# A hybrid block on one core: three raw weight buffers instead of two, and high priority for the copies between seven half-size products

## The chip, the core and the metric

The kernel runs on one core of a Trainium2 chip. The metric is the time of one execution in device microseconds (us), the median of several. The core has engines that work side by side, each through its own queue of instructions in a fixed order: PE (TensorE, matrix products; its weight loads are listed as PEld), DVE (VectorE), ACT (ScalarE), POOL (GpSimd) and SP (SyncE, which here only issues transfers). Engines wait for each other through semaphores. A page or an answer of the profile writes "A <- B" for "A stood idle until B was done".

## The reference

528 tokens (16 learnt meta tokens and 512 inputs) of width 1024 go through one block. With `z = rms_norm(h) @ w_in` cut into eight parts:

```python
u_rnn, u_gate, q, k, v, g_ret, ga, gb = jnp.split(z, IN_SPLITS, axis=-1)
xr = causal_dwconv(u_rnn, rnn_conv_w[l], rnn_conv_b[l])
hr = rg_lru(xr, ...)                      # recurrence over time, width 1280
o_a = hr * jax.nn.gelu(u_gate)
o = retention(rotary(q), rotary(k) * RET_DK ** -0.5, v)   # 4 heads, keys 256, values 512
o_b = head_rms(o) * jax.nn.silu(g_ret)
mixed = sigmoid(ga) * (o_a @ w_branch_rnn) + sigmoid(gb) * (o_b @ w_branch_ret)
h = h + mixed @ w_out
up = causal_dwconv(rms_norm(h) @ w_up, fconv_w, fconv_b)
gate, val = jnp.split(up, 2, axis=-1)
h = h + (gelu(gate) * val) @ w_down
out = rms_norm(h)[:, N_META:]
```

Everything is float32, and the weights come to some 100 MB. Their products are what the time goes into.

## The kernel before, in words

**Products.** PE multiplies in float16. Each float32 matrix is split in a high part (rounded to float16) and a low part (what is left), and a product is the sum of three: high by high, high by low and low by high. The split of a tile is two instructions in `split` (L91 to L94): ACT writes the high part (L92) and DVE the low one (L93), after ACT. So each weight passes three stages before PE can use it: a transfer into a raw buffer, a split on ACT, a split on DVE.

**Weights as units.** The weights are cut into units of 128x2048 float32 (1 MB; those of `w_branch_rnn` 640 KB), listed in the order of their use. `unit_load` takes a tile `raw` from the pool `wraw` (L59, two buffers) and issues its transfer on SP through `load` (L98 to L104), which keeps all weight loads in the order in which they were asked for. The float16 tiles `wt` (128x2x1024) come from the pool `wsp` (L60, ten). A raw buffer is free again when DVE has split the last of it; the load that is to fill it waits for that at the head of SP's queue, and everything that SP has to issue behind it waits as well.

**When splits are issued.** The program calls `tick` at many places between products. Each call issues at most one step of the list, a split or the sums below, as long as the tiles needed for the units ahead don't pass `ahead`. `emit_step` (L292 to L297) first makes sure that raw loads have been asked for up to one unit past the unit whose step it issues (`u + 2`).

**Seven half-size products.** Twenty units (gates `g_ret`, `ga`, `gb`, and `w_branch_ret`) use a scheme with seven products of half-size blocks in place of eight. Their weights are prepared by `fast_steps` (L237 to L275): two cuts are split as they are (B11, then B21 with B22), then three additions on DVE change the raw buffer in place (L256 to L258), then two more cuts (T1 with T3, T4 with T2) are split from the result. `fast_products` (L859 to L902) does the seven products, in accumulators of 257 columns, `pa`, `pe` and `pb`:

1. B11 into `pa`; `keep` (L871, L872) copies `pa` to the first half of `kept` on ACT.
2. T3 into `pe`.
3. T2, added on top in `pa`; `keep` copies `pa` to the second half of `kept`.
4. B21 into `pb`, and an addition with `kept` on DVE (L889).
5. T1, added on top in `pa`; `keep` copies to `last`; an addition on DVE (L893).
6. B22, added on top in `pa`; the gate function reads it (L905).
7. T4, added on top in `pe`; an addition on DVE (L900), and the gate function of the other half.

So before the products 3, 5 and 6 PE has to wait until ACT has copied `pa`, and the product in between is what covers that copy. For a unit of gates a product is 12 matmuls of 128x128 by 128x257, for `w_branch_ret` 24. L867 is the line of all of these matmuls; their inputs are `xs` and `xh` for the gates and `ob` for the second branch, and `pm` (L418) is an ordinary product of the first branch, 60 matmuls, which are woven in between.

**The order of instructions.** Up to `order.close()` (L736) the instructions of PE, ACT and DVE stand in the order in which the program issues them. Behind that, a scheduler chooses for each engine among what is ready by its own estimate, in the order of the program unless a part is given high priority. What is ready depends on the buffers as well, so the number of raw buffers changes the order too.

**The run of the work.** Up to about 140 us come the norm, the recurrence's projections and the recurrence; to 230 us queries and keys with their rotary multiplications (L759 to L761); to 425 us scores, values, retention and the gates of heads 0 to 2 (`gated`); from 420 to 644 us the mix (`mix_unit`, `gate_unit` for head 3, `mix_products`); then `w_out` with the residual `h` (L1186 loads it, L1193 loads the gain `gffn`), the second norm, `w_up` with its convolutions, `w_down` and the last norm.

Of the kernel before, what the change touches and what calls it, by code (L numbers as in the profile page):

```python
# [10 lines left out]
AF = mybir.ActivationFunctionType  # L11
# [40 lines left out]
def hybrid_block_kernel(ctx, tc, x, meta, norm_mix_g, w_in, conv_w, conv_b, rg_a_w, rg_a_b,  # L52
                        rg_x_w, rg_x_b, lam, w_brnn, w_bret, w_out, norm_ffn_g, w_up,
                        fconv_w, fconv_b, w_down, norm_final_g, rope_t, decay_t, out):
    nc = tc.nc
    const = ctx.enter_context(tc.tile_pool(name="const", bufs=1))
    xp = ctx.enter_context(tc.tile_pool(name="xp", bufs=4))
    pieces = ctx.enter_context(tc.tile_pool(name="pieces", bufs=46))
    wraw = ctx.enter_context(tc.tile_pool(name="wraw", bufs=2))  # L59
    wsp = ctx.enter_context(tc.tile_pool(name="wsp", bufs=10))  # L60
    work = ctx.enter_context(tc.tile_pool(name="work", bufs=8))
    small = ctx.enter_context(tc.tile_pool(name="small", bufs=4))
# [11 lines left out]
    def acc(name):  # L74
        return psum["acc"].tile([P, 2, 512], F32, name=name, tag="acc")

    def bank(name):
        return psum["bank"].tile([P, 512], F32, name=name, tag="bank")
# [9 lines left out]
    def wtile(name):  # L88
        return work.tile([P, T], F32, name=name, tag="w")
# [17 lines left out]
    def kmaj(w, k0, nk, c0, ncol):  # L107
        return w[k0 * P:(k0 + nk) * P, c0:c0 + ncol].rearrange("(k p) c -> p k c", p=P)

    units = []  # L110

    def unit(nk, ncol, parts, fast=False):
        units.append((nk, ncol, parts, fast))
        return len(units) - 1
# [3 lines left out]
    for i in range(5):  # L118
        u = unit(8, 256, [(0, 0, kmaj(w_in, 0, 8, o_ur + 256 * i, 256))])
# [65 lines left out]
    loaded = []  # L185

    def unit_load(cuts=1):

        nk, ncol, parts, fast = units[len(loaded)]
        raw = wraw.tile([P, 2048], F32, name="raw")  # L190
        n = nk * ncol
        rv = raw[:, :n].rearrange("p (k c) -> p k c", k=nk)
        for k0, c0, ap in parts:
            load(rv[:, k0:k0 + ap.shape[1], c0:c0 + ap.shape[2]], ap)
        loaded.append(len(loaded))
        if fast:
            return fast_steps(rv, nk // 2, ncol // 2)
        hk = nk // 2
        hn = hk * ncol
        tiles = []  # L200

        def step(i, c):
            def run():
                if c == 0:
                    tiles.append(wsp.tile([P, 2, 1024], F16, name="wt"))
                sl = slice(c * hn // cuts, (c + 1) * hn // cuts)
                split(tiles[i][:, 0, sl], tiles[i][:, 1, sl], raw[:, i * hn:(i + 1) * hn][:, sl], SW)
            return run

        wviews.append(lambda a, k, c0, m: tiles[k // hk][:, a, k % hk * ncol + c0:k % hk * ncol + c0 + m])  # L210
        return [step(i, c) for i in range(2) for c in range(cuts)]
# [66 lines left out]
    last_keep = [None]  # L278
# [12 lines left out]

    def emit_step():  # L292
        u, run = steps[done[0]]
        while len(loaded) < min(u + 2, len(units)):
            queue(unit_load())
        run()
        done[0] += 1  # L297

    def queue(new):
        steps.extend((len(loaded) - 1, run) for run in new)  # L300

    def get(u):
        current[0] = max(current[0], u)
        while len(loaded) <= u:
            queue(unit_load())
        while done[0] < len(steps) and steps[done[0]][0] <= u:
            emit_step()
        return wviews[u]

    def tick(n=1, late=True):  # L310


        for _ in range(n):
            if done[0] == len(steps):
                if len(loaded) == len(units):
                    return
                queue(unit_load())
            u = steps[done[0]][0]
            if sum(unit_tiles(i) for i in range(current[0], u + 1)) > ahead[0]:
                return  # L320
            if gating[0] and not late and hasattr(steps[done[0]][1], "late"):
                return
            emit_step()
# [292 lines left out]
    def conv_product(n):  # L616
        u, col = u_ur[n]
        if n in early:
            ps = early.pop(n)
            project_half(ps, get(u), col, xf, HR, 1)  # L620
        else:
            ps = acc("ps")
            project(ps, get(u), col, xf, HR, KD)
        return ps
# [46 lines left out]
    for n in range(NR):  # L671
        ps = conv_product(n)
# [41 lines left out]
    for n in range(NR):  # L714
        ps = acc("ps")
        u, col = u_ug[n // 2], (n % 2) * P
# [142 lines left out]
    def fast_products(ws, src, func, finish):  # L859


        last_k = 4 * len(ws) - 1

        def product(ps, wf, xf_, first=False):
            for k in range(last_k + 1):
                for aw, ax in SPLIT:
                    nc.tensor.matmul(ps[:, :257], ws[k // 4](wf, aw, k % 4), src(xf_, ax, k),  # L867
                                     start=first and k == 0 and (aw, ax) == (0, 0), stop=k == last_k and aw == 1,
                                     skip_group_check=True)

        def keep(dst, ps):  # L871
            last_keep[0] = nc.scalar.activation(dst, ps[:, :257], AF.Copy).ins  # L872

        kept, last = wtile("kept"), wtile("last")
        g0, g1 = wtile("g0"), wtile("g1")
        h0, h1 = slice(0, 257), slice(257, TQ)
        pa = bank("pa")
        product(pa, "B11", "A11", True)
        keep(kept[:, h0], pa)
        yield  # L880
        pe = bank("pe")
        product(pe, "T3", "F7", True)
        yield
        product(pa, "T2", "F6")
        keep(kept[:, h1], pa)
        yield
        pb = bank("pb")
        product(pb, "B21", "A12", True)
        nc.vector.tensor_tensor(g0[:, h0], pb[:, :257], kept[:, h0], op=ALU.add)  # L889
        yield  # L890
        product(pa, "T1", "F5")
        keep(last[:, h0], pa)
        nc.vector.tensor_tensor(g1[:, h1], pe[:, :257], last[:, h0], op=ALU.add)  # L893
        yield
        product(pa, "B22", "F3")
        func(g1[:, h0], pa[:, :257], -1.0, 0)
        func(g1[:, h1], g1[:, h1], -1.0, 257)
        finish(1, g1)
        product(pe, "T4", "A22")
        nc.vector.tensor_tensor(g0[:, h1], pe[:, :257], kept[:, h1], op=ALU.add)  # L900
        func(g0[:, :TQ], g0[:, :TQ], 1.0, 0)
        finish(0, g0)  # L902
# [215 lines left out]
    def branch(us, src, nk):  # L1118
        ps = acc("pm")
        project(ps, get(us.pop(0)), 0, src, HH, nk)  # L1120
        tick(2)
        return ps[:, :, :257]
# [21 lines left out]
    for i in range(2):  # L1144
# [5 lines left out]
        ps = branch(u_ba, oa_of, NR)  # L1150
# [525 lines left out]
```

## Time and profile before

| | |
|---|---|
| median of three runs | 1068.25 us (1067.45 to 1068.45) |
| the profiled execution, first to last instruction (span) | 1066.5 us |
| PE busy | 1048.0 us, 98% of the span |
| DVE busy | 853.2 us, 80% |
| ACT busy | 587.9 us, 55% |
| granted TensorE clock | 1.00 in all stretches, 0.99 in the last |
| bytes read | 108.04 MB, 103 GB/s over the span |

For the profiled execution itself nothing but its span is known, which is 1.75 us under the median. A row of a timeline has the start in us, the duration, the engine, the line, the operation, output <- input with shapes, and in brackets the idle time in front of it with what ended that; neighbours of one kind are put together (x12), and then the duration runs from the first start to the last end. In the table of stretches the columns are the stretch, its length, then the busy time (and count) of PE, PEld, DVE, ACT and POOL, the clock, the share of the transfer engines and GB/s.

### The profile page before, as it was taken

What the parts mean: (1) busy time and instruction counts of PE and PEld (TensorE: products, weight loads), DVE (VectorE), ACT (ScalarE), POOL (GpSimd) and SP (SyncE); (2) the same over time, 40 slices, a digit from 0 to 9 for tenths busy, and PEclk for the clock granted to TensorE, in tenths of its full rate; (3) what the DMA queues carried; (4) which work ended last, traced back from release to release, by engine and by line L of the source; (5) the groups of instructions that cost most, each with busy time, mean ns of one, the idle gap of its engine ahead of it and who ended that gap; (6) DMA issues with size and microseconds to landing.
All of it is one profiled execution on the core that took longest, in us unless ns stands there. A gap on an engine that the chain in (4) does not pass through costs nothing.

```text
span 1066.5 us, 20995 instructions
## 1 busy us (share of the span) xinstructions
PE 1048.0 (98%) x8995; PEld 851.1 (80%) x8995; DVE 853.2 (80%) x1301; ACT 587.9 (55%) x927; POOL 6.9 (1%) x20
## 2 busy tenths in 40 slices
PE   8999999999999999999999999999999999999997
PEld 6888888865685858887888885588888888888884
DVE  6884799998577878877797776479989897988965
ACT  8568954434364747655554454366566465454442
POOL 2000000000000000000000000000000000000000
PEclk9999999999999999999999999999999999999999
DMA  8341243431022312334433365032432324214322
GB/s 255 104 133 42 80 139 119 160 120 40 2 85 75 120 40 65 119 100 119 129 105 119 115 202 179 1 119 80 159 111 88 119 81 133 67 60 138 101 81 79
DMA packets 108989, 111.49 MB, mean 105 GB/s; under 512 B 5610, under 2 KB 100560, under 8 KB 108896
## 3 DMA queue, kind: packets, MB, share of 16 engines
q1 hardware_dynamic: 108448, 109.74, 32.0%
q8 instruction: 70, 1.15, 0.4%
q10 hardware_dynamic: 160, 0.27, 0.1%
q0 software_dynamic: 288, 0.14, 0.1%
q14 instruction: 23, 0.19, 0.1%
HBM read 108.04 MB, written 2.10 MB: 103 GB/s over the span
## 4 chain that ended last, share of the span: by engine, by line
PE 76%; DVE 13%; ACT 6%; DMA 2%; issue 2%; ACTq 0%; DVEq 0%
PE ps L418 31%; PE P L1512 9%; PE pa L867 7%; PE ps L930 6%; PE ps L1235 4%; DVE wt L93 4%; PE pe L867 3%; PE ps L431 3%; PE pm L418 2%; PE ps L953 2%; PE pa L1399 2%; ACT wt L92 2%; PE pb L867 2%; DVE rnn L665 1%; PE pe L1399 1%
## 5 line engine op out<-in xcount | busy, mean ns | idle before, releaser
L418 PEld LDWEIGHTS <-wt 128*128 128x128 f16 x3840 | 373.2, 97 | 58.2 <-DVE t L759 1.4
L93 DVE SCALAR_TENSOR_TENSOR wt<-raw,wt 128x1024 f16<-128x1024 f32 (+2 forms) x278 | 303.0, 1105 | 58.6 <-ACT wt L92 57.9
L92 ACT ACTIVATE wt<-raw 128x1024 f16<-128x1024 f32 (+2 forms) x278 | 261.4, 962 | 155.7 <-DVE raw L258 30.0
L867 PEld LDWEIGHTS <-wt 128*128 128x128 f16 x2016 | 195.0, 97 | 38.0 <-issue 11.2
L418 PE MATMUL ps<-x2h,wt 128*128 128x258 f16 x1184 | 181.2, 273 | 0.0
L418 PE MATMUL ps<-xh,wt 128*128 128x257 f16 (+2 forms) x1056 | 163.8, 275 | 1.1 <-DVE t L759 1.1
L418 PE MATMUL ps<-x2l,wt 128*128 128x258 f16 x592 | 113.2, 272 | 0.0
L418 PE MATMUL ps<-xl,wt 128*128 128x257 f16 (+2 forms) x528 | 102.2, 275 | 0.0
L1512 PE MATMUL P<-wt,act 128*128 128x256 f16 x792 | 88.3, 273 | 0.0
L1512 PEld LDWEIGHTS <-act 128*128 128x128 f16 x792 | 77.5, 98 | 9.0
L1377 DVE SCALAR_TENSOR_TENSOR cv<-ps,vt,cv 128x512 f32<-128x512 f32 x80 | 59.8, 748 | 22.7 <-ACT cv L1375 21.8
L867 PE MATMUL pa<-xs,wt 128*128 128x257 f16 x576 | 71.6, 273 | 5.1 <-ACT kept L872 4.7
L930 PE MATMUL ps<-wt,xh 128*128 128x512 f16 x256 | 76.1, 379 | 0.4 <-DVE v L93 0.4
L418 PE MATMUL pm<-oa,wt 128*128 128x257 f16 x480 | 55.3, 274 | 0.0
L1375 ACT ACTIVATE cv<-ps,vt,vt 128x512 f32<-128x512 f32 x40 | 30.9, 773 | 34.5 <-PE ps L418 33.8
L930 PE MATMUL ps<-wt,xl 128*128 128x512 f16 x128 | 48.5, 379 | 0.0
L930 PEld LDWEIGHTS <-xh 128*128 128x128 f16 x256 | 24.8, 98 | 29.3 <-issue 0.7
L256 DVE TENSOR_TENSOR raw<-raw 128x1024 f32<-128x1024 f32 x39 | 47.5, 1219 | 0.6
L867 PE MATMUL pa<-ob,wt 128*128 128x257 f16 x384 | 45.7, 274 | 2.0 <-ACT kept L872 1.4
L1235 PE MATMUL ps<-wt,mx 128*128 128x512 f16 x192 | 44.3, 378 | 0.0
L1399 PEld LDWEIGHTS <-wt 128*128 128x128 f16 x336 | 32.6, 97 | 4.4
L1235 PEld LDWEIGHTS <-mx 128*128 128x128 f16 x192 | 17.7, 98 | 18.4
(293 smaller groups left out, 1409.0 us busy)
## 6 DMA issues: line engine op xcount, KB each, us to landing
raw<-in_w_in SPq DMA_DIRECT2D x40, 1024.0 KB, 4.9
raw<-in_w_up SPq DMA_DIRECT2D x24, 1024.0 KB, 5.2
raw<-in_w_down SPq DMA_DIRECT2D x48, 256.0 KB, 3.5
raw<-in_w_branch_ret SPq DMA_DIRECT2D x16, 512.0 KB, 4.7
raw<-in_w_branch_rnn SPq DMA_DIRECT2D x8, 640.0 KB, 4.6
raw<-in_w_out SPq DMA_DIRECT2D x4, 1024.0 KB, 6.2
xin<-in_x SPq DMA_DIRECT2D x4, 512.0 KB, 5.6
raw<-in_w_in SPq DMA_DIRECT2D x4, 512.0 KB, 8.1
```

The costliest lines, as they stand in the source:

```text
L92: a = nc.scalar.activation(hi, src, AF.Copy, scale=s)
L93: b = nc.vector.scalar_tensor_tensor(lo, src, s, hi, op0=ALU.mult, op1=ALU.subtract)
L256: nc.vector.tensor_tensor(pair, pair, rv[:, :, right].rearrange("p (h k) c -> p h k c", h=2), op=ALU.add)
L418: nc.tensor.matmul(ps[:, hf, :n], w(aw, k, col, P), src(ax, k, c0, n), start=k == 0 and (aw, ax) == (0, 0), stop=k == nk - 1 and aw == 1)
L431: mm = nc.tensor.matmul(ps[:, hf, :n], w(aw, k, col, P), src(ax, k, c0, n), start=k == 0 and (aw, ax) == (0, 0), stop=k == KD - 1 and aw == 1)
L867: nc.tensor.matmul(ps[:, :257], ws[k // 4](wf, aw, k % 4), src(xf_, ax, k), start=first and k == 0 and (aw, ax) == (0, 0), stop=k == last_ ...
L930: nc.tensor.matmul(pb, xf(ax, k, XF + j0, nb), w(aw, k % 4, 0, 512), start=i == 0, stop=i == 23)
L1235: nc.tensor.matmul(ps[:, n], mx[k][:, a, c0:c0 + P], wo[k // 2](aw, k % 2, n * 512, 512), start=k == 0 and (a, aw) == (0, 0), stop=k == ks ...
L1375: nc.scalar.activation(vv_, src[:, :, 2:258], AF.Identity, scale=vt2[:, 96 + ch:97 + ch], bias=bias)
L1377: nc.vector.scalar_tensor_tensor(vv_, src[:, :, j:j + 256], vt2[:, 48 * j + ch:48 * j + ch + 1], vv_, op0=ALU.mult, op1=ALU.add)
L1399: nc.tensor.matmul(ps[:, :258], w(wf, aw, k), x2_form(xf_, ax, k), start=first and k == 0 and (aw, ax) == (0, 0), stop=k == 3 and aw == 1, ...
L1512: nc.tensor.matmul(pd[:, 256 * tt:256 * tt + 256], t[:, ax, c0 + tt * P:c0 + tt * P + P], w(wf, aw, i), start=q % 6 == 0 and tt == 0 and i ...
```

## The change

There are four edits. The pool of raw buffers gets a third buffer (8 KB more per partition). `emit_step` asks for loads up to two units past the one whose step it issues. The copies of `keep`, three in each of the twenty `fast_products`, are issued under high priority for the scheduler. The scratch space for the descriptors of POOL's own transfers is set to 4096 (it was left at its default). No arithmetic is changed, and no instruction but the order of them: ACT, DVE and SP get theirs in another order from about 140 us on, PE at one place.

```diff
-    wraw = ctx.enter_context(tc.tile_pool(name="wraw", bufs=2))
+    wraw = ctx.enter_context(tc.tile_pool(name="wraw", bufs=3))
...
     def emit_step():
         u, run = steps[done[0]]
-        while len(loaded) < min(u + 2, len(units)):
+        while len(loaded) < min(u + 3, len(units)):
             queue(unit_load())
         run()
         done[0] += 1
...
         def keep(dst, ps):
-            last_keep[0] = nc.scalar.activation(dst, ps[:, :257], AF.Copy).ins
+            with tc.high_priority():
+                last_keep[0] = nc.scalar.activation(dst, ps[:, :257], AF.Copy).ins
...
-    nc = bacc.Bacc("TRN2", target_bir_lowering=False, num_devices=1)
+    nc = bacc.Bacc("TRN2", target_bir_lowering=False, num_devices=1, dynamic_dma_scratch_size=4096)
```

The changed kernel has one line more: from L872 on its numbers are one higher (the copy is L873 there, the gate function L906).

## The prediction

> **What bounds the kernel now.** I read the page first, then the table of stretches, then the list of waits.
>
> ```profile
> span 1066.5 us, 20995 instructions
> ...
> PE 1048.0 (98%) x8995; PEld 851.1 (80%) x8995; DVE 853.2 (80%) x1301; ACT 587.9 (55%) x927; POOL 6.9 (1%) x20
> ```
> ```profile
> 425.00:520.00 95.00, 92.14 (x820) 80.09 (x820) 78.05 (x114) 57.24 (x88) 0.00 (x0) 1.00 0.38 113
> ...
> 650.00:760.00 110.00, 110.00 (x913) 79.84 (x912) 79.70 (x119) 57.86 (x104) 0.00 (x0) 1.00 0.31 99
> 760.00:950.00 190.00, 190.00 (x1712) 166.00 (x1711) 162.80 (x241) 105.25 (x156) 0.00 (x0) 1.00 0.31 101
> ```
>
> PE is busy for 1048.0 of 1066.5 us, so TensorE sets the time, and since the change takes no product away, all it can win is PE's idle time: 18.5 us in the whole span. From 650 to 950 us there is none (the PE column equals the stretch), while 425 to 520 us loses 2.9 us. So the branch products, before 650 us, are the place to look. The waits say for whom PE stands there.
>
> ```profile
> PE pa L867 <- ACT kept L872: 6.2, 8, 1.6
> ...
> ACT wt L92 <- DMA raw<-in_w_out: 6.7, 2, 5.9
> ...
> ACT wt L92 <- DMA raw<-in_w_branch_rnn: 3.7, 1, 3.7
> ```
> ```profile
> SPq L104 <- DVE wt L93: 818.0, 83, 56.6
> ```
>
> Columns: us in total, times, longest. PE loses 6.2 us in 8 waits for the copies into `kept`, which frees the accumulator `pa` for the next product. The copies are late because ACT is: it stands 6.7 us for w_out and 3.7 us for w_branch_rnn to arrive. Those loads are late because SP, for 818.0 us in all, stands with the next load in hand until DVE has split the last of a raw buffer. Hence the chain: raw buffer, load, split on ACT, copy on ACT, PE. Both halves of the change act on it.
>
> **The two long stalls that start with a load.** First the mix unit at 489 us.
>
> ```profile
> 469.47 12.57 SPq L104 DMA_DIRECT2D raw<-in_w_branch_rnn  x2
> ```
> ```profile
> 486.30 0.74 ACT L92 ACTIVATE wt<-raw 128x640 f16<-128x640 f32 x1 [3.66 <-DMA raw<-in_w_branch_rnn]
> ...
> 487.06 1.28 ACT L905 ACT_TABLE_LOAD   x1
> ...
> 488.68 0.37 ACT L872 ACTIVATE kept<-pa 128x257 f32<-128x257 f32 x1
> ...
> 489.10 1.49 PE L867 MATMUL pa<-xs,wt 128*128 128x257 f16 x12 [1.57 <-ACT kept L872]
> 489.10 2.64 PEld L867 LDWEIGHTS <-wt 128*128 128x128 f16 x24 [1.74 <-issue]
> ...
> 492.77 0.49 PE L867 MATMUL pa<-xs,wt 128*128 128x257 f16 x3 [0.86 <-ACT kept L872]
> ```
>
> ACT's rows of that unit, `last` of the unit before it to the second `kept`, before and after (wt is a split, g a gate, ob an output's split):
>
> ```order
> L872 ACTIVATE last<-pa 128x257
> L92 ACTIVATE wt<-raw 128x640
> L905 ACT_TABLE_LOAD
> L905 ACTIVATE g_5737<-g_5737 128x257
> L872 ACTIVATE kept<-pa 128x257
> L92 ACTIVATE wt<-raw 128x640
> L905 ACTIVATE g_5737<-pa 128x257
> L92 ACTIVATE wt<-raw 128x512
> L92 ACTIVATE wt<-raw 128x1024
> L92 ACTIVATE ob<-or_4796 128x514
> L905 ACTIVATE g_5736<-g_5736 128x514
> L872 ACTIVATE kept<-pa 128x257
> ```
> ```order
> L873 ACTIVATE last<-pa 128x257
> L92 ACTIVATE wt<-raw 128x640
> L906 ACT_TABLE_LOAD
> L906 ACTIVATE g_5739<-g_5739 128x257
> L873 ACTIVATE kept<-pa 128x257
> L92 ACTIVATE wt<-raw 128x512
> L906 ACTIVATE g_5739<-pa 128x257
> L92 ACTIVATE wt<-raw 128x1024
> L92 ACTIVATE ob<-or_4798 128x514
> L906 ACTIVATE g_5738<-g_5738 128x514
> L92 ACTIVATE ob_5554<-or_4797 128x257
> L873 ACTIVATE kept<-pa 128x257
> ```
>
> The last of the 128x640 splits has moved out from between the two copies, and the one that still stands ahead of the table load is now the second of its load. SP's row says that the two loads left at 469.47 and 481.67 (469.47 + 12.57, less the issue itself). With a third buffer a load waits for the split of the unit three back, which was done when its predecessor left; so the second load goes right behind the first and is there about 8 us before ACT's 482.6 (486.30 less its wait). The wait of 3.66 us goes, and the whole row of table load, gate and copy moves up by up to that much; PE needs it only 1.57 us earlier. What was hidden is late next? The copy would end near 482.6 + 0.74 + 1.28 + 0.33 (the gate) + 0.37 = 485.4, and PE asks at 487.4 (489.10 - 1.74), so 2 us of slack are left. Gain: the 1.57 us and PE's refill, which the weight loads show (1.74 in place of 1.57): 1.74. The second copy, 0.86 us late, had a 640 split ahead of it that is gone (0.7 us of queue) and starts from an ACT that is 2 us earlier, but has one more small ob row ahead: I take 0.9.
>
> The second place is the end of the mix, at 641 us.
>
> ```profile
> 622.34 0.37 SPq L104 DMA_DIRECT2D raw<-in_w_out  x1
> ...
> 631.32 2.98 SPq L104 DMA_DIRECT2D raw<-in_w_out  x2
> ...
> 638.58 2.00 ACT L92 ACTIVATE wt<-raw 128x1024 f16<-128x1024 f32 x2 [5.86 <-DMA raw<-in_w_out]
> ...
> 640.91 0.49 PE L867 MATMUL pa<-ob,wt 128*128 128x257 f16 x3 [1.42 <-ACT kept L872]
> ```
>
> SP's rows there, before and after (h is the residual, hs its small edge rows):
>
> ```order
> L104 DMA raw<-in_w_branch_ret 128x4x256 x4
> L104 DMA raw<-in_w_out 128x2x1024
> L1186 DMA h_7842<-in_x 128x1024 x2
> L1186 DMA h_7843<-in_x 128x1024 x2
> L104 DMA raw<-in_w_out 128x2x1024 x2
> ```
> ```order
> L104 DMA raw<-in_w_branch_ret 128x4x256 x4
> L104 DMA raw<-in_w_out 128x2x1024 x2
> L1187 DMA h_7844<-in_x 128x1024 x2
> L1187 DMA h_7845<-in_x 128x1024 x2
> L104 DMA raw<-in_w_out 128x2x1024 x2
> ```
>
> The second w_out load has passed the four h transfers. It leaves at about 622.7 in place of 631.32 and is there well before ACT asks for it at 632.7 (638.58 less 5.86). ACT's wait goes, the copy comes 3 us early, and PE wins 1.42 and the same refill of 0.17: 1.59.
>
> Here a rule stands against the change. The Trainium skill, page "Trainium Kernel Development and Optimization", section Best Practices, advises to double-buffer so that transfers overlap compute; two buffers were there already, and by that rule a third would add nothing: these three terms would be 0. The waits of 3.66 and 5.86 us in the rows above speak against it here.
>
> **The copies that pass one instruction.** At two places the copy stood behind one that did not need to be first.
>
> ```profile
> 407.22 0.64 ACT L905 ACTIVATE g<-g 128x514 f32<-128x514 f32 x1
> ...
> 408.18 0.49 PE L867 MATMUL pa<-xs,wt 128*128 128x257 f16 x3 [0.49 <-ACT kept L872]
> ```
> ```profile
> 543.59 0.62 ACT L92 ACTIVATE mx<-m 128x514 f16<-128x514 f32 x1
> 544.11 0.36 ACT L872 ACTIVATE kept<-pa 128x257 f32<-128x257 f32 x1
> ...
> 544.53 0.71 PE L867 MATMUL pa<-xs,wt 128*128 128x257 f16 x5 [0.60 <-ACT kept L872]
> ```
>
> In the order of after `kept` stands ahead of that gate at 407 us and ahead of that mx at 544 us. Starts are 0.52 us apart (543.59 to 544.11), so each copy comes 0.52 earlier: 0.5 and 0.5, of the 0.49 + 0.17 and 0.60 + 0.17 that PE lost. Behind them gate and mx come 0.4 us later, and their readers on DVE have no PE wait behind them.
>
> **What it costs.** The earlier loads make splits ready earlier, and the scheduler has put them ahead of copies. The clearest place is the first mix unit, at 422 us.
>
> ```profile
> 421.79 0.37 ACT L872 ACTIVATE kept<-pa 128x257 f32<-128x257 f32 x1
> ...
> 422.21 1.49 PE L867 MATMUL pa<-xs,wt 128*128 128x257 f16 x12 [0.20 <-ACT kept L872]
> ...
> 425.23 0.94 PE L867 MATMUL pa<-xs,wt 128*128 128x257 f16 x7 [0.53 <-ACT kept L872]
> ...
> 425.84 0.63 ACT L92 ACTIVATE wt<-raw 128x512 f16<-128x512 f32 x1 [0.67 <-DMA raw<-in_w_in]
> ```
>
> ACT's rows before and after, from the first 640 split to the second copy:
>
> ```order
> L92 ACTIVATE wt<-raw 128x640
> L905 ACTIVATE g_4925<-g_4925 128x514
> L92 ACTIVATE ob<-or_4241 128x514
> L92 ACTIVATE wt<-raw 128x640
> L92 ACTIVATE ob_4978<-or_4240 128x257
> L872 ACTIVATE kept<-pa 128x257
> L92 ACTIVATE ob<-y 128x514
> L92 ACTIVATE ob<-d 128x514
> L872 ACTIVATE kept<-pa 128x257
> ```
> ```order
> L92 ACTIVATE wt<-raw 128x640
> L906 ACTIVATE g_4927<-g_4927 128x514
> L92 ACTIVATE ob<-or_4243 128x514
> L92 ACTIVATE wt<-raw 128x640
> L92 ACTIVATE wt<-raw 128x512
> L92 ACTIVATE ob_4980<-or_4242 128x257
> L92 ACTIVATE wt<-raw 128x1024
> L873 ACTIVATE kept<-pa 128x257
> L92 ACTIVATE ob<-y 128x514
> L92 ACTIVATE ob<-d 128x514
> L873 ACTIVATE kept<-pa 128x257
> ```
>
> A 512 and a 1024 split now stand ahead of the first copy: 0.63 and 1.00 us (half of the 2.00 for two at 638.58). Their raw is not the one that ACT waits for at 425.84: that wait ended the load that left after 420.86, which with a third buffer leaves a step earlier, some 13 us. So the copy ends at 421.79 + 0.37 + 1.63 = 423.8. PE's own order gives way a little: six more `pb` and two `pm` matmuls of 0.11 us now come ahead of the second `pa` product, so PE asks at 422.9 (422.21 - 0.20 + 0.9) and stands 0.9. The second copy, with four `pm` ahead of its reader, is then on time. Before, the two cost 0.20 + 0.53 = 0.7. Net -0.2; from both sides, +0.7 if the splits find room in ACT's waits, -1.5 if the second copy is late too.
>
> ```profile
> 470.04 1.49 PE L867 MATMUL pe<-xs,wt 128*128 128x257 f16 x12
> ...
> 471.37 1.49 PE L867 MATMUL pa<-xs,wt 128*128 128x257 f16 x12
> ```
> ```profile
> 470.35 0.37 ACT L872 ACTIVATE kept<-pa 128x257 f32<-128x257 f32 x1
> ```
>
> A product of 12 matmuls takes 1.33 us (470.04 to 471.37). In this gate unit a 1024 split (1.00) has come between the last gate and the first copy: 470.35 + 1.00 + 0.37 = 471.7, asked for at 471.3. A new stall: -0.4 (0 to -1.0).
>
> ```profile
> 161.48 0.40 PE L418 MATMUL ps<-xh,wt 128*128 128x257 f16 x2 [1.12 <-DVE t L759]
> ```
> ```profile
> L93 DVE SCALAR_TENSOR_TENSOR wt<-raw,wt 128x1024 f16<-128x1024 f32 (+2 forms) x278 | 303.0, 1105 | 58.6 <-ACT wt L92 57.9
> ```
>
> At 161 us PE waits for DVE's rotary multiplications. In the new order DVE has one more split ahead of them (1.1 us, the mean of 1105 ns) and one multiplication less: between 0 and -1.1, of which I take about the middle, -0.5, since the multiplication is the shorter of the two.
>
> ```profile
> L371 DVE SCALAR_TENSOR_TENSOR xo<-h,rs,gffn x8: 744/748/753, 664.3 to 700.2; 128x512 f32<-128x512 f32 x8
> ...
> DMA to landing us min/median/max: 5.5/5.7/6.0
> ```
> ```profile
> 656.95 0.38 SPq L104 DMA_DIRECT2D raw<-in_w_up  x1
> ```
>
> SP sets four w_up loads ahead of gffn in place of two; the fourth gets its buffer when the third did before, at 656.95. Gffn then lands at about 657.4 + 5.7 = 663.1, first read at 664.3: hidden, cost 0 (to -0.3). PE has work there (110.00 of 110).
>
> **The sum.** 1.74 + 0.9 + 1.59 + 0.5 + 0.5 - 0.2 - 0.4 - 0.5 = 4.1 us. The profiled span is 1066.5, 1.75 under the median of 1068.25, and I carry that difference along: 1068.25 - 4.1 = 1064.1. With each cost at its two ends the gain is 1.9 to 6.3, so 1062.0 to 1066.4 for this case.
>
> **The rivals.** *All copies on time.* The eight waits hold 6.2 us, with eight refills of 0.17 that is 7.6; no new ones: 1060.6. Against it stand the splits put ahead of copies. 0.08.
>
> *Loads were no limit.* The rule above: the three load terms give 0, the copies' 1.0 stays: 1067.2, no difference that can be measured. It would need the weight tiles, not raw buffers, to hold ACT up at 489 and 641; the rows name the load there. 0.13.
>
> *Slower: a split that isn't ready holds a copy.* ACT takes its rows in order. The pool of ten weight tiles has not grown, so a split that comes a unit earlier may have to wait until PE has read a tile out. At 422 us that would put the 512 split where it stood, 425.84, and the copy at 425.84 + 0.63 + 1.00 + 0.37 = 427.8 against 422.9: 4.9 us in place of 0.7, -4.2. The load terms go too, since their splits wait for tiles likewise; with -0.4 and -0.5 and the 1.0 of the copies: +4.1, 1072.4. It decides at whether that split starts before about 422.4. For it: the shared pool. Against it: the rows at 425.84, 486.30 and 638.58 all name a DMA and none a product of PE. 0.07.
>
> *Descriptor space.* The change cuts the scratch for POOL's transfers, and nothing in the trace shows what is left over.
>
> ```profile
> 12.12 0.51 POOL L581 DMA_DIRECT2D v<-in_norm_ffn_g  x1 [1.96 <-DMA v<-in_rnn_conv_w]
> ```
> ```profile
> L583 PE MATMUL ptv<-ident,v x1: 273/273/273, 24.0 to 24.0; 128*128 128x128 f32 x1
> ...
> DMA to landing us min/median/max: 4.9/5.7/6.2
> ```
>
> The last of POOL's nine transfers leaves at 12.12 and lands by 18; PE reads at 24.0. One more wait for a landing (5.7) is hidden, two make 12.1 + 11.4 + 5.7 = 29.2 and eat 5.2 us, all that was won: about 1069. 0.04.
>
> **How the numbers follow.** The forecast's own case has 0.68. A measurement of this kernel can tell 0.2%, 2.1 us, from no change, so faster means under 1066.1. Of the 0.68, 0.03 lies above that. Faster: 0.65 + 0.08 = 0.73. Same: 0.03 + 0.13 + 0.04 = 0.20. Slower: 0.07. The range takes the forecast's case and the rival without load terms whole, 1062.0 to 1067.2, and is drawn to 1061.5 and 1067.8 for the parts of the sum that were read to a tenth only: 0.81.
>
> **What would show it.** In the profile after: PE's busy time as before, `pa` waiting for `kept` some 4 us less; no ACT wait for w_branch_rnn near 482 and none for w_out near 632; a wait of about 0.9 us near 422 and 0.4 near 471; the rotary wait at 161 us grown to 1.6. Wrong would be: ACT waits named for PE or for weight tiles ahead of these copies, a wait of several us near 422, or PE idle after 650 us.

## The result and the profile after

The changed kernel takes 1064.96 us in the median of 7 runs (1064.85 to 1065.39), the kernel before 1067.62 in 7 runs (1066.99 to 1070.32), the three of above among them. The ratio is 0.9975, with a 95% interval of 0.9966 to 0.9984: 2.7 us are gone, and the interval allows 1.7 to 3.6. The forecast was 4.1 us from 1068.25. The profiled execution of after took 1064.96 us, its span is 1063.2, which is 3.3 less than before's 1066.5.

The page of after, then the stretches that the prediction showed:

```profile
span 1063.2 us, 20995 instructions
...
PE 1047.6 (99%) x8995; PEld 851.7 (80%) x8995; DVE 853.1 (80%) x1301; ACT 587.5 (55%) x927; POOL 6.9 (1%) x20
```
```profile
425.00:520.00 95.00, 94.09 (x842) 82.02 (x840) 80.20 (x117) 57.80 (x89) 0.00 (x0) 1.00 0.38 115
650.00:760.00 110.00, 110.00 (x928) 81.23 (x927) 78.32 (x118) 56.86 (x103) 0.00 (x0) 1.00 0.30 98
```

PE's work is the same (1047.6 us against 1048.0), and its idle time has shrunk from 18.5 to 15.6 us. The stretch from 425 to 520 us loses 0.9 us in place of 2.9, and from 650 to 760 us PE still has no gap. The list of waits of after (us in total, times, longest):

```profile
ACT wt L92 <- DMA raw<-in_w_in: 6.5, 2, 5.5
...
PE pa L867 <- ACT kept L873: 2.5, 3, 1.2
```

ACT's waits for w_out and for w_branch_rnn are no longer in the list, those for w_in went from 25.7 us in 12 to 6.5 in 2, and PE waits for `kept` 2.5 us in place of 6.2. What has not fallen is SP's standing for a split to free a raw buffer: 844.3 us, 818.0 before. That total is no measure of what a buffer is worth; the waits of ACT and PE are. First the mix unit at 489 us, ACT's rows of after:

```profile
484.19 0.73 ACT L92 ACTIVATE wt<-raw 128x640 f16<-128x640 f32 x1
484.94 1.28 ACT L906 ACT_TABLE_LOAD   x1
486.23 0.42 ACT L906 ACTIVATE g<-g 128x257 f32<-128x257 f32 x1
486.56 0.37 ACT L873 ACTIVATE kept<-pa 128x257 f32<-128x257 f32 x1
```

The split ahead of the table load waits for nothing, the copy starts at 486.56 (before: 488.68), and neither this product nor the next one (493 us) has a wait. What took their place stands earlier. PE's rows of after at the four places where it waits more than before:

```profile
161.91 0.40 PE L418 MATMUL ps<-xh,wt 128*128 128x257 f16 x2 [1.65 <-DVE t L759]
...
194.69 0.39 PE L418 MATMUL ps<-xh,wt 128*128 128x264 f16 x2 [0.32 <-DVE t L759]
...
424.52 0.60 PE L867 MATMUL pa<-xs,wt 128*128 128x257 f16 x4 [1.23 <-ACT kept L873]
...
472.97 0.49 PE L867 MATMUL pa<-xs,wt 128*128 128x257 f16 x3 [0.79 <-ACT kept L873]
```

The waits of PE at all places that differ, in us, read from the same rows of six kernels (0 stands for no wait there; "buffers" and "priority" are the two halves of the change run alone, "kept only" and "best" two later kernels, all below):

| place | before | priority | buffers | after | kept only | best |
|---|---|---|---|---|---|---|
| 161 and 194 | 1.12 | 1.11 | 1.96 | 1.97 | 1.98 | 1.12 |
| 408 | 0.49 | 0 | 0.49 | 0 | 0 | 0 |
| 422 and 425 | 0.73 | 1.25 | 0.73 | 1.25 | 1.26 | 1.26 |
| 458 | 0.11 | 0.30 | 0 | 0 | 0 | 0 |
| 472 | 0 | 0 | 0.18 | 0.79 | 0.17 | 0.18 |
| 489 and 493 | 2.43 | 3.02 | 0 | 0 | 0 | 0 |
| 544 | 0.60 | 0.08 | 0.60 | 0.08 | 0.08 | 0.08 |
| 641 | 1.42 | 0 | 0 | 0 | 0 | 0 |
| sum | 6.90 | 5.76 | 3.96 | 4.09 | 3.49 | 2.64 |

From before to after that is 2.8 us; with the refills of about 0.17 that came or went with each wait it is 3.2 of the 3.3 by which the spans differ; the other 0.1 lies ahead of 161 us. The place at 458 us (a wait of 0.11 with its refill, 0.28 won) was not foreseen. So the places account for the two profiles. Whether they account for the medians is what the experiments had to say.

### The profile page after: what moved, and what is told of

Read it like the earlier page. It is cut to its first block, busy times and chain, and to the rows that moved or that the text cites. A ratio compares the mean times of both kernels' runs of the same rounds, so it can differ in the third digit from the quotient of the medians.

```text
span 1063.2 us, 20995 instructions
## 1 busy us (share of the span) xinstructions
PE 1047.6 (99%) x8995; PEld 851.7 (80%) x8995; DVE 853.1 (80%) x1301; ACT 587.5 (55%) x927; POOL 6.9 (1%) x20
## 4 chain that ended last, share of the span: by engine, by line
PE 74%; DVE 16%; ACT 7%; issue 2%; DMA 0%; ACTq 0%; DVEq 0%
PE ps L418 26%; PE P L1513 9%; PE pa L867 9%; PE ps L931 6%; DVE wt L93 5%; PE pe L867 4%; PE ps L1236 4%; PE ps L431 3%; PE pm L418 3%; PE ps L954 2%; PE pb L867 2%; PE pa L1400 2%; ACT wt L92 2%; DVE rnn L665 1%; PE pe L1400 1%
## 5 line engine op out<-in xcount | busy, mean ns | idle before, releaser
L1236 PEld LDWEIGHTS <-mx 128*128 128x128 f16 x192 | 17.6, 98 | 18.5
```

The source lines that it names most:

```text
L1236: nc.tensor.matmul(ps[:, n], mx[k][:, a, c0:c0 + P], wo[k // 2](aw, k % 2, n * 512, 512), start=k == 0 and (a, aw) == (0, 0), stop=k == ks ...
```

## The experiments

**The two halves of the change.** Theory: the loads carry the gain and the copies pay for themselves. Rival: the copies carry it, or each half alone does nothing.

The copies under high priority, and nothing else:

```diff
         def keep(dst, ps):
-            last_keep[0] = nc.scalar.activation(dst, ps[:, :257], AF.Copy).ins
+            with tc.high_priority():
+                last_keep[0] = nc.scalar.activation(dst, ps[:, :257], AF.Copy).ins
```

> Before, with high priority for the copies alone (two buffers, one unit ahead). Theory A (the two halves of the change are separate, and priority moves three of the sixty copies, two of them ones that PE waits for): PE's waits near 408 and 544 us shrink by 0.52 each, the rest stays as before, so 1.0 us less than before. Rival B (priority is what brings the copies at 489, 492 and 641 in time): most of the 4.3 us of those three places go, so 3 us or more less than before, and the waits there are gone.

The three other edits (third buffer, asking two units ahead, scratch), without the priority:

```diff
         def keep(dst, ps):
-            with tc.high_priority():
-                last_keep[0] = nc.scalar.activation(dst, ps[:, :257], AF.Copy).ins
+            last_keep[0] = nc.scalar.activation(dst, ps[:, :257], AF.Copy).ins
```

> The change without the high priority (three buffers, two units ahead). Theory A: the waits at 489, 492 and 641 are gone (1.73 + 1.03 + 1.58), 408 and 544 stand as before, the new waits near 161, 194, 424 and 471 are there as in the change (-2.5): about 2 us less than before, 1 us more than the change. Rival B: the waits at 489, 492 and 641 come back, and with the new ones the time is 1 to 3 us over before.

Priority alone: 1066.99 us against 1067.85 of before, 0.9987 (0.9978 to 0.9996). Buffers alone: 1065.05, 0.9973 (0.9963 to 0.9984), which is the whole of the change (0.9975). The priority adds nothing that can be measured to the buffers. That priority alone came out 0.9 under before, near the 1.0 of theory A, is luck: 408 and 544 us went as the theory said, but 0.5 was lost at 422, and the waits at 458, 489 and 493 did not stay as they were. The table says why the priority adds nothing: it takes 0.5 us away at 408 and 0.5 at 544, and gives 0.5 back at 422 and 425 and 0.6 at 472. PE's row of the kernel with buffers alone shows the wait at 424, 0.71 where after has 1.23:

```profile
424.78 0.94 PE L867 MATMUL pa<-xs,wt 128*128 128x257 f16 x7 [0.71 <-ACT kept L872]
```

So the cost of 0.5 at 422 and 425 us is not that of the early splits, for which the prediction had 0.2, but that of the priority.

**What takes back the 0.5 of 408 us.** The rows of ACT and PE of after at 408 us show that the copy did come early and that PE started without a wait:

```profile
408.14 0.39 ACT L873 ACTIVATE kept<-pa 128x257 f32<-128x257 f32 x1
408.40 0.65 ACT L906 ACTIVATE g<-g 128x514 f32<-128x514 f32 x1
```
```profile
408.58 0.60 PE L867 MATMUL pa<-xs,wt 128*128 128x257 f16 x4
```

The table of stretches for the 16 us behind it (PE, PEld, DVE, ACT busy), before and after:

```profile
408.00:424.00 16.00, 15.62 (x155) 13.73 (x155) 15.96 (x30) 10.61 (x22) 0.00 (x0) 1.00 0.27 82
```
```profile
408.00:424.00 16.00, 15.29 (x152) 13.34 (x150) 15.96 (x29) 12.32 (x24) 0.00 (x0) 1.00 0.25 79
```

DVE is busy for 15.96 of 16 us in both. Within the stretch, ACT's gate stands for an addition of DVE, by as much as was won at 408 (in before this gate had no wait):

```profile
420.65 0.63 ACT L906 ACTIVATE g<-g 128x514 f32<-128x514 f32 x1 [0.53 <-DVE g L901]
```

Theory: DVE bounds this stretch, and whatever PE wins at its start it waits at its end, where the chain is DVE's addition, the gate, five splits (two of outputs, three of weights), the copy. Rival: PE's own work or the splits bound it. Two experiments. The first gives PE five more matmuls at 408 us, in a bank that the following product starts anew:

```diff
+        for _ in range(extra):
+            nc.tensor.matmul(pb[:, :257], ws[0]("B21", 0, 0), src("A12", 0, 0), start=True, stop=False,
+                             skip_group_check=True)
...
-        return fast_products([get(u_gr[h][i])], x_forms, gate_func(AF.Silu), finish)
+        return fast_products([get(u_gr[h][i])], x_forms, gate_func(AF.Silu), finish, 5 if (h, i) == (2, 1) else 0)
```

> The change, with five matmuls more on PE just behind the copy's place at 408 us (the first matmul of a product into pb, issued five times more and then overwritten: 5 x 0.11 = 0.55 us of PE work that leads nowhere). Theory E (from 408 to 424 us DVE has no idle time and sets when the copy at 424 comes, so PE's 0.52 us won at 408 is given back there): the wait at 424 falls from 1.40 to about 0.85, and the time is that of the change within 0.2. Rival F (PE and the copies set the pace there, and what is won at 408 is kept): the wait at 424 stays at 1.40 and the time is 0.55 over the change.

The second leaves one addition of 128x514 on DVE out there:

```diff
-            if d > 0:
+            if d > 0 and (h, d) != (3, 2):
                 nc.vector.tensor_add(ssum[:, :TQ], ssum[:, :TQ], sq[:, :TQ])
```

> The change without one of DVE's additions (the third square sum of head 3 leaves out one of its four terms), a 0.69 us row between 408 and 424 us, starts 0.60 apart; ACT's order is as in the change. Theory E: the copy at 424 comes 0.6 earlier, the wait there falls from 1.40 to about 0.8, and the time falls by up to 0.6, less what is given back at 472. Rival F (ACT's two splits ahead of the copy set its time): the wait at 424 stays at 1.2 to 1.4, and the time is that of the change within 0.2.

PE's rows, first with the five matmuls, then without the addition:

```profile
424.35 0.82 PE L867 MATMUL pa<-xs,wt 128*128 128x257 f16 x6 [0.58 <-ACT kept L873]
```
```profile
424.43 0.82 PE L867 MATMUL pa<-xs,wt 128*128 128x257 f16 x6 [0.58 <-ACT kept L873]
```

The wait falls from 1.23 to 0.58 both times, for opposite reasons. Five more matmuls cost nothing: 1064.85 (0.9974, 0.9963 to 0.9985) against 1064.96; PE merely stood less. One DVE addition less brings 0.65: 1064.31 (0.9967, 0.9955 to 0.9980). The profiled execution of that kernel took longer than this median, 1064.87, because it was 0.56 us behind that of after at all places up to 412 us; from 424 us on it is 0.09 ahead, so the 0.65 is seen in the profile too. DVE bounds the stretch; shown from both sides.

**The stall at 641 us.** The prediction gave it 1.59, the second largest term. In the profile of priority alone, SP's order there is that of before, yet the stall was gone. Theory: what the profile of before shows at 641 is one slow landing in one execution, not a cost of every run. Rival: it is there in the typical run. The third buffer for that one unit, all else as before but the scratch, and the scratch alone:

```diff
     wraw = ctx.enter_context(tc.tile_pool(name="wraw", bufs=2))
+    wraw3 = ctx.enter_context(tc.tile_pool(name="wraw3", bufs=1))
...
-        raw = wraw.tile([P, 2048], F32, name="raw")
+        u = len(loaded)
+        raw = (wraw3 if u == u_out[1] else wraw).tile([P, 2048], F32, name="raw")
```

> Before, with a third raw buffer that only the second w_out unit uses, and the smaller descriptor scratch; no high priority. The orders of PE and DVE are those of before. Theory G (the wait at 641 depends on the landing of one load, 7.2 us after its issue in the profile of before and 4.8 in that of priority alone, so it stands in some executions only): the wait at 641 is gone, all others are as before, and the median falls by 0.3 to 1.3. Theory A, strictly (it is there in each execution): the median falls by 1.6. Rival H (later transfers h and hs are delayed behind the w_out load): PE idle behind 644 us, and no gain.

```diff
-    nc = bacc.Bacc("TRN2", target_bir_lowering=False, num_devices=1)
+    nc = bacc.Bacc("TRN2", target_bir_lowering=False, num_devices=1, dynamic_dma_scratch_size=4096)
```

> Before with the smaller descriptor scratch alone. Theory: POOL's nine transfers leave and land as before (last issue near 12.1, first read at 24.0 us), and the time is that of before within 0.3. Rival (the scratch is too small for nine transfers in flight): POOL waits 5 us or more for a landing before 12 us, and PE waits near 24 us.

The buffer for w_out: 1067.61, 1.0004 (0.9995 to 1.0013). The scratch: 1067.72, 1.0002 (0.9993 to 1.0011). Neither moves the time. The loads of 620 to 634 us, from issue to landing, in before (three) and in the kernel with the scratch alone (two), whose order of instructions is before's:

```profile
DMA to landing us min/median/max: 5.1/7.2/7.3
```
```profile
DMA to landing us min/median/max: 5.0/5.2/5.5
```

And the issue and ACT's wait in the latter:

```profile
631.82 2.98 SPq L104 DMA_DIRECT2D raw<-in_w_out  x2
...
636.82 1.06 ACT L92 ACTIVATE wt<-raw 128x1024 f16<-128x1024 f32 x1 [3.60 <-DMA raw<-in_w_out]
```

The same load, the second of w_out, is asked for at the same point and lands 5.0 us after its issue here, 7.3 in before (631.32 to 638.58). ACT waits 3.60 in place of 5.86, the copy is in time, and PE does not stand at 641. Of the three profiles with before's order at this place one has the stall and two have not; and where it can't come about (the third buffer for w_out) the median is the same as with the scratch alone, 0.1 us apart. The fall of 0.3 to 1.3 that theory G expected did not come: the interval allows at most 0.5. So the 1.58 us stood in the profile and hardly in the median.

**Where the third buffer is needed.** Theory: two loads do the work (w_branch_rnn of 489 us and the second w_out), and a third buffer for those alone avoids the costs at 161, 194 and 472. Rival: the load in every place counts. Once for these two units, once for every third unit from the mix on, so that the part of the program before it stays as it was. Both are the changed kernel with two common buffers and one of its own for those units:

```diff
-    wraw = ctx.enter_context(tc.tile_pool(name="wraw", bufs=3))
+    wraw = ctx.enter_context(tc.tile_pool(name="wraw", bufs=2))
+    wraw3 = ctx.enter_context(tc.tile_pool(name="wraw3", bufs=1))
...
+    own_third = (u_ba[5], u_out[1])
...
-        raw = wraw.tile([P, 2048], F32, name="raw")
+        u = len(loaded)
+        raw = (wraw3 if u in own_third else wraw).tile([P, 2048], F32, name="raw")
```

> The change, with a third raw buffer that only two units use: the sixth of w_branch_rnn (read at 489 us) and the second of w_out (read at 641 us); all others have two. Theory A (what the third buffer wins is these two loads, what it costs is the splits elsewhere): the gains at 489, 492, 641, 408 and 544 stay and the waits at 161, 194, 424 and 471 are as before: 5.3 us less than before, 2 to 2.6 less than the change. Rival D (the gain needs all loads to run ahead): the waits at 489 and 641 stay at 1 us or more, and the time is between the change and before.

The second, against the first:

```diff
-        raw = (wraw3 if u in own_third else wraw).tile([P, 2048], F32, name="raw")
+        raw = (wraw3 if u >= u_ga[0] and (u - u_ga[0]) % 3 == 2 else wraw).tile([P, 2048], F32, name="raw")
```

> The change, with the third raw buffer used by every third unit from the first gate unit of the mix on, and two buffers before that. Theory A (the splits that come earlier delay DVE's rotary multiplications): PE's waits at 161 and 194 us go back to 1.28 and to none, all behind 400 us stays as in the change: 1.0 us less than the change, some 3.7 to 4.2 less than before. Rival C (those two waits have another cause, such as the clock or transfers in flight): no difference to the change.

For two units: 1065.34, 0.9974 (0.9965 to 0.9984). The theory failed: ACT's wait at 486 went, but DVE now had one 640 split ahead of its two additions (L893 at 485.29 and L897), and PE waited for the second of them. And ACT stood 1.02 us for the next load, one of w_in, which has only two buffers here; the splits behind it and the second copy are late by as much, and PE waited 1.03 for that copy. The three engines' rows:

```profile
484.55 0.81 DVE L94 SCALAR_TENSOR_TENSOR wt<-raw,wt 128x640 f16<-128x640 f32 x1
...
485.62 0.42 DVE L897 TENSOR_TENSOR g<-pe,last 128x257 f32<-128x257 f32 x1
485.95 0.81 DVE L94 SCALAR_TENSOR_TENSOR wt<-raw,wt 128x640 f16<-128x640 f32 x1
```
```profile
487.79 0.63 ACT L93 ACTIVATE wt<-raw 128x512 f16<-128x512 f32 x1 [1.02 <-DMA raw<-in_w_in]
```
```profile
486.09 0.27 PE L870 MATMUL pe<-xh,wt 128*128 128x257 f16 x1 [0.65 <-DVE g L897]
...
492.59 0.60 PE L870 MATMUL pa<-xs,wt 128*128 128x257 f16 x4 [1.03 <-ACT kept L876]
```

So rival D is right in part: the load behind these two has to run ahead as well.

For every third unit from the mix on: 1064.39, 0.9968 (0.9955 to 0.9980), 0.6 under the change. PE's wait at 161 us is 1.11 again and that at 194 is gone; the rest is as in after. So in the rotary part the third buffer costs 0.85 us of waits, 1.0 with a refill, and brings nothing. That the median fell by 0.6 and not by the 1.0 of theory A is within what the executions differ by: ahead of 161 us the profiled execution was 0.3 behind that of after. PE reaches its wait there between 160.2 and 160.8 us in the 14 profiles of this document, with two buffers as with three.

**Asking ahead or having room.** The change with the asking depth of before, so that only the buffer is left:

```diff
-        while len(loaded) < min(u + 3, len(units)):
+        while len(loaded) < min(u + 2, len(units)):
```

> The change, with loads asked for one unit ahead as before (u + 2), and three buffers. ACT's, DVE's and PE's orders are those of the change; on SP three loads stand elsewhere. Theory L (a load waits for its buffer, not for its being asked for, so the third buffer alone does it): the time of the change within 0.2. Rival M (without being asked for earlier the third buffer stands empty): the waits at 489 and 492 come back, 2 to 2.7 over the change.

1065.10, 0.9981 (0.9972 to 0.9989), against 1067.19 of before beside it: as the change, within 0.14 us. With three buffers the depth does nothing; SP stood with a load in hand for a buffer, and the buffer is what it needed. Two buffers with the greater depth were not run.

**The new stall at 472 us.** ACT's rows of after from `last` on:

```profile
461.77 0.37 ACT L873 ACTIVATE last<-pa 128x257 f32<-128x257 f32 x1
462.03 0.62 ACT L92 ACTIVATE ob<-d 128x514 f16<-128x514 f32 x1
464.49 1.28 ACT L906 ACT_TABLE_LOAD   x1 [1.83 <-DVE g L894]
```

The priority has put `last` ahead of the split `ob<-d`, and behind them the table load stands 1.83 us for DVE's addition. Theory: that order makes the table load wait, and what hangs on it, by way of ACT's 512 split and DVE's sums down to the copy at 472.55, is late. Rival: it is the 1024 split that the buffers put ahead of the copy, as predicted. The priority for `kept` alone:

```diff
-        def keep(dst, ps):
-            with tc.high_priority():
+        def keep(dst, ps, first=True):
+            with tc.high_priority() if first else nullcontext():
...
-        keep(last[:, h0], pa)
+        keep(last[:, h0], pa, False)
```

> The change, with the high priority only on the copies into kept, not on those into last. ACT's order differs from the change by one swap, at 462 us: the split ob<-d stands ahead of last again, and so last stands right ahead of the table load; PE's and DVE's orders are the same. Theory I (that swap makes the table load of 1.28 us wait for DVE, which puts the second part of the gate, DVE's sums and the copy at 472 back by 0.6): the table load comes right behind last without a wait, the wait at 472 falls from 0.96 to about 0.35, and the time is 0.5 to 0.6 under the change. Rival J (the wait at 472 comes from the splits ahead of the copy alone): it stays at 0.96, and the time is that of the change within 0.2.

ACT's rows, then PE's:

```profile
462.49 0.37 ACT L873 ACTIVATE last<-pa 128x257 f32<-128x257 f32 x1
462.88 1.28 ACT L906 ACT_TABLE_LOAD   x1
464.64 0.42 ACT L906 ACTIVATE g<-g 128x257 f32<-128x257 f32 x1 [0.48 <-DVE g L894]
```
```profile
472.56 0.71 PE L867 MATMUL pa<-xs,wt 128*128 128x257 f16 x5 [0.17 <-ACT kept L873]
```

The table load now runs while DVE adds, and PE's wait is 0.17, what the buffers alone leave. 1064.44, 0.9974 (0.9965 to 0.9984), 0.66 under the kernel of the asking depth, which ran beside it. The traces of the two kernels agree in the order of PE, DVE and SP throughout, and in ACT's but for this swap; with it the wait for DVE's addition L894 passes from the gate (0.48) to the table load (1.83).

**A better version.** The third buffer from the mix on and the priority for `kept` only, once with the DVE addition of the stretch from 408 to 424 us moved to POOL, and once without that move:

```diff
-                nc.vector.tensor_add(ssum[:, :TQ], ssum[:, :TQ], sq[:, :TQ])
+                (nc.gpsimd if (h, d) == (3, 2) else nc.vector).tensor_add(ssum[:, :TQ], ssum[:, :TQ], sq[:, :TQ])
```

> Three corrections together: the third raw buffer from the mix on only (as in e3), high priority on the copies into kept only (as in e9), and the one addition that e6 left out done on POOL instead of DVE, so that the output is whole. If they add up: 0.6 (e3) + 0.6 (e9) + 0.65 (e6) under the change, about 1063.1. Rival K (POOL's addition is slow enough, or shares enough with DVE, that the gain of e6 is lost): 0.65 more, about 1063.8.

> As e10, with the addition left on DVE: the third raw buffer from the mix on only, and high priority on the copies into kept only. Theory K (on POOL the addition took 2.75 us, and one of DVE's rows that ran beside it took 1.44 in place of 0.69, so POOL's help was worth nothing): the wait at 424 stays at 1.40, as in e10, and the time is that of e10 within 0.2, 1063.6. Rival N (POOL's help was worth its 0.6 elsewhere): 1064.1 or more.

With POOL: 1063.57, 0.9966 (0.9952 to 0.9979). Without: 1063.39 (1063.31 to 1063.48), 0.9964 (0.9950 to 0.9977) against 1067.18: the fastest of all, 3.8 us under before, and 1.2 (by the ratios) to 1.6 (by the medians) under the change. The intervals of the two ratios overlap, as they do for every step of 0.6 us here; the runs of the two kernels do not (1063.48 at most, 1064.85 at least). The move to POOL brought nothing. In the profile, what the better version wins over the change is the waits at 161 and 194 us and the one at 472, 1.6 us. POOL's row and DVE's rows beside it, then the same DVE rows where the addition is on DVE (the kernel with every third unit):

```profile
412.42 2.75 POOL L964 TENSOR_TENSOR ssum<-ssum,sq 128x514 f32<-128x514 f32 x1 [399.89 <-ACT sq L962]
```
```profile
413.34 0.69 DVE L259 TENSOR_TENSOR raw<-raw 128x512 f32<-128x512 f32 x1
...
414.27 1.44 DVE L260 TENSOR_TENSOR raw<-raw 128x512 f32<-128x512 f32 x1
415.64 0.41 DVE L896 TENSOR_TENSOR g<-pe,last 128x257 f32<-128x257 f32 x1
```
```profile
413.32 0.69 DVE L964 TENSOR_TENSOR ssum<-ssum,sq 128x514 f32<-128x514 f32 x1
...
414.97 0.69 DVE L260 TENSOR_TENSOR raw<-raw 128x512 f32<-128x512 f32 x1
415.58 0.42 DVE L896 TENSOR_TENSOR g<-pe,last 128x257 f32<-128x257 f32 x1
```

DVE has one instruction of 0.69 less, but its addition of L260 beside POOL's takes 1.44 in place of 0.69, and the addition behind it starts at 415.64 and 415.58. The Trainium skill, page "SBUF — State Buffer", section Who interferes with whom, says that a DVE instruction with two SBUF inputs and a GpSimd instruction that reads SBUF contend. The trace agrees in one row, which is stretched by 0.75 us; another addition with two inputs that ran beside POOL's, L259, kept its 0.69, and why that one did is open.

## Why the prediction was right, and where not

The sign, the place and the order of size were right: the loads carry the gain, none of the rivals came about, and the time lies 0.9 us above the forecast. That the time came so near is in part luck. The forecast started from 1068.25, which is 0.6 above the median of 7 runs, and it took 1.59 off for a stall that the median hardly has; the two errors go against each other, and the gain, 2.7 in place of 4.1, is further off than the time. The two ends of the sum don't come out of its terms either: with each cost at its two ends they give 1.3 to 5.9, not 1.9 to 6.3, and 1.9 comes out only with the term of 161 us left at its middle. Point by point:

- **489 and 493 us (1.74 and 0.9)**: right. ACT's wait of 3.66 us went, nothing took its place, and PE won 1.73 and 1.03.
- **641 us (1.59)**: the mechanism is right in the profile (the load of after leaves at 620.66, and ACT has no wait for w_out), the size is wrong for the time that is measured. It was read off a single execution in which the load took 7.3 us; where it takes 5.0 PE does not stand there. Worth nothing in the median that can be measured.
- **408 and 544 us (0.5 each)**: both came, 0.52 each. At 544 it stayed. At 408 it was given back at 424, and here a step failed: "their readers on DVE have no PE wait behind them". PE's waits at 422 and 425 are behind them, since DVE is full from 408 to 424 us. The prediction looked at the next instruction, not at what bounds the stretch.
- **422 and 425 us (−0.2)**: 0.53 was lost, but by the priority, not by the early splits: with the buffers alone the two places lose 0.73, as before. There it went nearly as the prediction had it: the copy 1.4 us later (it had 1.6), one wait of 0.71 (0.9) and the second copy on time.
- **472 us (−0.4)**: 0.96 with its refill. Of the wait of 0.79, 0.18 belongs to the split that the prediction named. The rest is the table load behind `last`, a copy whose move was not looked at.
- **161 us (−0.5)**: right, 0.53. At 153 us DVE has a 1024 split (1.14 us to the next start) where it had a multiplication of the recurrence (0.61). **194 us**: the same thing 33 us later, 0.49 with its refill, not foreseen. DVE has three 1024 splits ahead of the multiplications there where it had two.
- **Gffn (0)**, **descriptor space** (its own case): no trace of either; the scratch alone is worth 0.0 (1.0002).

"Loads were no limit" was given 0.13: the Trainium skill ("Trainium Kernel Development and Optimization", section Best Practices) advises to double-buffer, and the prediction read this as saying that a third buffer has nothing to bring, which the page does not say. Here the buffers alone brought 2.8 us (1067.85 to 1065.05), so the measurement decides against that reading.

What stays open: the medians move more than the places. Against the profile of the scratch alone (the order of before without the stall at 641) the spans can be followed place by place: priority alone wins 0.16 us, the change 2.2. The medians say 0.9 and 2.7. The profiled execution of the scratch alone was the fastest of its 11 (1067.14 us, 0.6 under that kernel's median), so what the medians have on top lies in the other executions of before. These lie further apart: 12 of the 103 runs of before, of the scratch alone and of the third buffer for w_out took 1069.5 us or more, and all 72 runs of the kernels that have the third buffer at 489 us took under 1066. Before's median itself is 1067.85 beside one set of runs and 1067.19 beside another, and so the gain of what is in effect the same kernel is 2.8 us in one set (buffers alone) and 2.1 in another (the asking depth). This looks like a time that hangs on when loads land, but which loads is open: ACT's waits for w_in, 25.7 us in before and 6.5 in after, are not enough, since the best version has 19.4 us of them and its five runs lie within 0.17. No profile shows one of those 12 runs, so this is argued, not shown.

## What to carry to other kernels

A wait for a load that is seen in one profile is worth what a second profile of the same order still shows; before it becomes a term, see whether it depends on how long one load took to land. A copy that comes half a microsecond earlier is a gain only if the engines between it and PE's next wait have room: look at the busy time of every engine in that stretch, and where one is full, cut there. When instructions get priority, list for each which ones it passes, table loads among them, and give it only to those that PE waits for.

## What was not expected of the hardware

- The same load of 1 MB, asked for at the same point of the program, landed 5.0 us after its issue in one execution (631.82 to 636.82, where ACT's wait ends) and 7.3 in another (631.32 to 638.58).
- A table load takes 1.28 us here and nothing more: at 484.94 it starts right behind the split before it, and the gate starts at 486.23, 1.29 later. All 31 table loads of that profile take as long, and behind all but the last the next instruction starts within 0.06 us. The Trainium skill, page "ScalarE: Activation LUTs", section What ACT_TABLE_LOAD costs, has 1283 ns for the load, which the trace shows, and a drain of 1380 ns, which none of them shows.
- An addition of 128x514 takes 2.75 us on POOL beside a busy DVE and 0.69 on DVE.
